# Three of four weight sums on VectorE, and block loads on SyncE's queue, in a Strassen-Winograd feed-forward kernel

## The chip, the cores and the metric

The kernel runs on one NeuronCore of a Trainium2 chip. The metric is device time in microseconds (us) of one execution. Engines: TensorE (PE, with its weight loads as PEld), VectorE (DVE), ScalarE (ACT), GpSimd (POOL) and SyncE (SP, which here only issues DMAs). POOL issues DMAs too, and it alone can issue a DMA that adds to what lies at the destination (an accumulating DMA).

## The reference

An encoder of two layers. Each layer is a feed-forward block, a mixer (gated linear attention beside softmax attention) and a second feed-forward block, on 512 tokens and 16 learned ones (528 columns; 512 in the last block). Everything is float32.

```python
def swiglu(x, w_gate, w_up, w_down):
    return (jax.nn.silu(x @ w_gate) * (x @ w_up)) @ w_down
...
    for l in range(DEPTH):
        h = h + 0.5 * swiglu(rmsnorm(h, norm_gains[l, 0]),
                             ffn_w_gate[l, 0], ffn_w_up[l, 0], ffn_w_down[l, 0])
        h = h + mixer(rmsnorm(h, norm_gains[l, 1]), w_in[l], ...)
        h = h + 0.5 * swiglu(rmsnorm(h, norm_gains[l, 2]),
                             ffn_w_gate[l, 1], ffn_w_up[l, 1], ffn_w_down[l, 1])
    return rmsnorm(h, final_norm)[:, N_META:]
```

D_MODEL is 1024 and D_FF is 2816. The change touches only how the weights of the feed-forward blocks get ready; the mixer's code stays.

## The kernel before

*Layout.* Activations lie transposed, features on the 128 partitions, tokens along the free dimension. A matmul takes a weight tile of 128 x 128 as the stationary operand and half the tokens (264 or 256 columns) as the moving one. To keep float32 accuracy each weight tile and each activation is split in two float32r parts, `hi` (a ScalarE copy, line 259) and `lo` (a VectorE subtraction, line 260), and each product is three matmuls: hi x hi, hi x lo, lo x hi.

*Sets.* A feed-forward block multiplies 2 x 2 blocks by the Strassen-Winograd scheme: seven products, named 1 to 7, where the plain way has eight. The weights of one such scheme are a set `i`: four blocks 11, 12, 21, 22 of 128 x 1024 floats (512 KB) in DRAM (`win`). Products 1, 2 and 4 take the blocks 11, 12 and 22 as they are; the other four take weight sums:

- s3 = B21 - B11, product 7
- s2 = B22 + s3, product 6
- s1 = B21 + B22, product 5
- s4 = s2 - B12, product 3

Of the 15 sets of each of the four feed-forward blocks, 0 to 10 (`NPAIR` = 11) are gate and up ("pairs" of column tiles; line 566 is their matmul), and 11 to 14 are down (line 680). Pairs run in three groups of 4, 4 and 3. After each of the first two groups come two down sets; the third group's down products are done the plain way (line 433).

*How a sum is formed.* `sums` is called when block 11 is fetched (product "1") and when product "2" is made. s3: ScalarE writes -B11 into a "long" buffer (`negative`, line 198), and POOL adds B21 from DRAM by an accumulating DMA (line 203; `s<-win` in the profile). s2: POOL loads B22 into a "short" buffer (line 193, `w<-win`) and adds s3 to it by another accumulating DMA, SBUF to SBUF (`w<-s`). s1: POOL loads B21 into a short buffer and adds B22 from DRAM. s4: in pairs 2 to 10 VectorE subtracts B12 from s2 when product 6 is made (line 228); in the other sets ScalarE negates B12 and POOL adds s2 (`s<-w`). The raw block 12 is kept in its buffer until line 228 has read it.

*Order.* `ffn_steps` writes the products out in order; in the middle of a group it is 1 of the next pair, then 7, then 2 of the next pair, 4, 3, then 6 and 5 of the next pair. `use` makes `hi` and `lo` up to two products ahead and fetches eight ahead. Raw blocks have three buffers and go by SP's queue; long sums have three buffers (`wsa`), short ones two (`wsb`), by POOL's queue. Within these wishes a list scheduler of the compiler sets the order on each engine and queue by its own estimate of times; on the chip each engine and each queue takes its instructions strictly in that order. A line 688 on VectorE adds a finished down product from PSUM to the residual `h` and so frees the bank.

Of the kernel before, what the change touches and what calls it, by code (L numbers as in the profile page):

```python
# [14 lines left out]
ALU = mybir.AluOpType  # L15
# [128 lines left out]
NPAIR = FF // P // 2  # L144
# [21 lines left out]
class Weights:  # L166
# [21 lines left out]
    def block(self, f, i, name, pool=None, tag="raw"):  # L188

        w = (pool or self.raw).tile([P, SLAB], F32, tag=tag, name=f"w{name}_{f[0]}{f[1]}_{i}")  # L190
        first = f + (i, name) == (0, 0, 0, "11")
        for a in np.split(np.arange(SLAB), 2 if first else 1):
            (self.nc.gpsimd if pool else self.nc.sync).dma_start(w[:, a[0] : a[-1] + 1], self.dram(f, i, name)[:, a[0] : a[-1] + 1])  # L193
        return w

    def negative(self, f, i, name, w):
# [8 lines left out]
    def sums(self, f, i, product, w):  # L205


        got = self.summed
        if product == "1":
            s3 = self.negative(f, i, "s3", w)  # L210
            self.add(s3, self.dram(f, i, "21"))
            s2 = self.block(f, i, "22", self.short, "wsb")
            self.add(s2, s3)
            got[f, i, "7"], got[f, i, "6"] = s3, s2
        if product == "12"[(f, i) in OPENING]:
            s1 = self.block(f, i, "21", self.short, "wsb")
            self.add(s1, self.dram(f, i, "22"))
            got[f, i, "5"] = s1
        late = 2 <= i < NPAIR
        if product == "2" and not late:  # L220
            s4 = self.negative(f, i, "s4", w)
            self.add(s4, got[f, i, "6"])
            got[f, i, "3"] = s4
        if product == "2" and late:
            self.kept = w
        if product == "6" and late:
            s4 = self.long.tile([P, SLAB], F32, tag="wsa", name=f"s4_{f[0]}{f[1]}_{i}")
            self.nc.vector.tensor_tensor(s4, w, self.kept, ALU.subtract)
            got[f, i, "3"] = s4
# [15 lines left out]
    def make(self, upto):  # L245
        nc = self.nc
        while self.made < min(upto, len(self.loads)):
            self.fetch(self.made + 1)
            s = self.made
            load = self.loads[s]  # L250
            w = self.raws.pop(s, None)
            if w is None:
                w = self.summed.pop(load)
            hi = self.hi_pool.tile([P, SLAB], F32R, tag="whi", name=f"whi{s}")
            lo = self.lo_pool.tile([P, SLAB], F32R, tag="wlo", name=f"wlo{s}")
            for a in np.split(np.arange(SLAB), 2 if s == 0 else 1):
                cs = slice(a[0], a[-1] + 1)
                with self.tc.issue_after(self.behind) if self.behind else nullcontext():
                    nc.scalar.copy(hi[:, cs], w[:, cs])  # L259
                nc.vector.tensor_tensor(lo[:, cs], w[:, cs], hi[:, cs].bitcast(F32), ALU.subtract)  # L260
            self.got[s] = (hi, lo)
            self.got.pop(s - 12, None)
            self.made += 1
            if not isinstance(load, int) and (load[2] in "26" or load[2] == "1" and load[:2] in OPENING):
                self.sums(*load, w)
# [31 lines left out]
def build(tc, ctx, xt, wts, win, par, w2, const, umask, out):  # L297
    nc = tc.nc
# [16 lines left out]
    def open_pools(side, psum=(), **bufs):  # L315
        made[0] += 1
        out = {}
        for n, b in bufs.items():
            space = dict(space=bass.MemoryType.PSUM) if n in psum else dict(side=side)
            out[n] = tc.alloc_tile_pool(name=f"{n}_{made[0]}", bufs=b, reuse_waits="tile", **space)  # L320
        slots.update(out)
        return out
# [218 lines left out]
    def ffn(l, f, norm, done, following):  # L541

        x, rs, up, n = norm.x, None, None, live[0]
        w = n // 2
        pools = open_pools("left", psum=("s2",), c=4, s2=2)
        made, hid, sums, raw, sets = {}, {}, {}, {}, {}
        risen = iter(range(KC))

# [540 lines left out]
        norm.pools = open_pools("right", **{"x": dict(x=16), "xc": dict(xc=8)}[kind])  # L1089

    def block_pools():
        pools = open_pools("left", wsa=3, wsb=2)
        W.long, W.short = pools["wsa"], pools["wsb"]
        return pools

# [89 lines left out]
    def finish_chunk(c):  # L1185
        fin.square(c)
        gain(c, slice(0, SEQ))

    def ending(sums, operand, rs):

        table("abs_reciprocal_sqrt_and_small")
# [44 lines left out]
    first = Norm(G_NORM)  # L1236
    operand_pools(first, "xc")
    bp = [block_pools()]
    nc.sync.dma_start(h(1), xt[:, 1])
    first.pair(0)  # L1240
# [15 lines left out]
    for l in range(DEPTH):  # L1256
        a, b, c = norms[3 * l : 3 * l + 3]
        ffn(l, 0, a, b.chunk, lambda: operand_pools(b, "x"))
        close_pools(bp.pop())
        mixer(l, b, c.chunk_of_pair, lambda: (operand_pools(c, "xc"), bp.append(block_pools())))  # L1260
        if l < DEPTH - 1:
            d = norms[3 * l + 3]
            ffn(l, 1, c, d.pair_of, lambda: operand_pools(d, "xc"))
        else:
            ffn(l, 1, c, None, lambda: None)
# [72 lines left out]
```

## Time and profile before

| | |
|---|---|
| median of three runs | 2267.75 us (2262.52 to 2270.09) |
| profiled execution | 2280.39 us, span 2278.6 us, mean granted TensorE clock 0.989 |
| PE, PEld busy | 2188.9 us, 2088.3 us |
| DVE, ACT, POOL busy | 1685.8 us, 1262.7 us, 246.1 us |
| w<-win by SP; by POOL | 179 DMAs, median 5.4 us to landing; 180, 6.1 us |
| s<-win, w<-s, s<-w by POOL | 60, 60 and 24 DMAs, median 7.6, 5.2 and 7.7 us to landing |

Busy time is the union of an engine's instructions; what ends an idle time ("<-") is inferred from semaphores. "w" is a loaded block or a short sum, "s" a long sum, "whi" and "wlo" the two parts, "c" and "g" activations of the feed-forward block, "ss" PSUM.

### The profile page before, as it was taken

The numbers are of one execution on the slowest core, as the hardware profiler recorded it, in microseconds if no ns is written. First come the engines' busy times: TensorE is split into PE (matmuls) and PEld (weight loads), VectorE is DVE, ScalarE is ACT, GpSimd is POOL, SyncE is SP. The second block draws the span as 40 slices with busy tenths as digits, with TensorE's granted clock in tenths as the row PEclk, the third lists the DMA queues.
The fourth block names the chain that finished last, engine by engine and source line by source line (L and its number), as shares of the span: only waits on it lengthen the run. The fifth ranks groups of instructions, "written<-read, shape, count | busy, mean of one in ns | idle before, by whom it ended". The sixth has DMA issues, their size and how long they took to land.

```text
span 2278.6 us, 40100 instructions
## 1 busy us (share of the span) xinstructions
PE 2188.9 (96%) x16506; PEld 2088.3 (92%) x16506; DVE 1685.8 (74%) x2607; ACT 1262.7 (55%) x1831; POOL 246.1 (11%) x328
## 2 busy tenths in 40 slices
PE   6989999999999999999999899999999999999998
PEld 6989999989999999998999898998888888999997
DVE  7776867586886678667788768575878767786867
ACT  7545545354785565454575455454547846555553
POOL 1211110000000011111012111100000001121110
PEclk9999999999999999999999999999999999999999
DMA  8877873212113477777668777832121135887871
GB/s 241 217 198 185 203 195 106 77 54 66 47 38 112 129 189 187 204 192 202 175 148 208 201 193 178 201 114 86 56 74 47 47 121 136 216 213 213 204 204 65
DMA packets 94951, 338.68 MB, mean 149 GB/s; under 512 B 10544, under 2 KB 12976, under 8 KB 94768
## 3 DMA queue, kind: packets, MB, share of 16 engines
q0 software_dynamic: 46656, 169.89, 33.9%
q1 hardware_dynamic: 46160, 163.73, 21.2%
q8 instruction: 130, 2.13, 0.4%
q10 hardware_dynamic: 1952, 2.50, 0.3%
q14 instruction: 53, 0.43, 0.1%
HBM read 289.94 MB, written 2.10 MB: 128 GB/s over the span
## 4 chain that ended last, share of the span: by engine, by line
PE 60%; DMA 13%; DVE 12%; issue 8%; ACT 6%; POOL 1%; SPq 0%; DVEq 0%; POOLq 0%; ACTq 0%
PE ss L566 24%; PE mm L433 14%; DMA w<-win 10%; PE ss L433 9%; PE ss L680 4%; DVE wlo L260 3%; PE sm L433 2%; DMA w<-s 2%; ACT whi L259 1%; PE sm L1041 1%; DMA s<-w 1%; PE ss L1016 1%; POOL w L203 1%; ACT s L198 1%; PE sm L1057 1%
## 5 line engine op out<-in xcount | busy, mean ns | idle before, releaser
L566 PE MATMUL ss<-xc,whi 128*128 128x264 f32 (+1 forms) x4928 | 905.6, 285 | 25.6 <-ACT whi L259 13.4
L566 PEld LDWEIGHTS ss<-xc,whi 128*128 128x128 f32 x4928 | 767.1, 189 | 30.8 <-ACT whi L259 14.3
L566 PE MATMUL ss<-xc,wlo 128*128 128x264 f32 (+1 forms) x2464 | 702.1, 285 | 3.7 <-DVE wlo L260 3.7
L260 DVE TENSOR_TENSOR wlo<-w,whi 128x1024 fp32r<-128x1024 f32 (+1 forms) x301 | 365.5, 1217 | 155.6 <-ACT whi L259 155.4
L566 PEld LDWEIGHTS ss<-xc,wlo 128*128 128x128 f32 x2464 | 466.3, 189 | 5.8 <-DVE wlo L260 5.8
L259 ACT CAST whi<-w 128x1024 fp32r<-128x1024 f32 (+1 forms) x301 | 313.0, 1047 | 143.1 <-DMA w<-win 34.0
L433 PE MATMUL mm<-x,whi 128*128 128x264 f32 (+1 forms) x1712 | 385.3, 315 | 0.0
L433 PEld LDWEIGHTS mm<-x,whi 128*128 128x128 f32 x1712 | 279.2, 189 | 16.5 <-issue 1.0
L680 PE MATMUL ss<-g,whi 128*128 128x264 f32 (+1 forms) x1280 | 250.9, 294 | 29.2 <-DVE h L688 17.2
L433 PE MATMUL mm<-x,wlo 128*128 128x264 f32 (+1 forms) x856 | 266.7, 316 | 0.0
L680 PEld LDWEIGHTS ss<-g,whi 128*128 128x128 f32 x1280 | 206.8, 196 | 35.9 <-ACT whi L259 19.5
L259 ACT CAST whi<-raw 128x1024 fp32r<-128x1024 f32 x126 | 132.1, 1049 | 164.4 <-PE mm L433 103.0
L570 ACT COPY c<-ss 128x528 f32<-128x528 f32 (+1 forms) x132 | 78.5, 595 | 224.3 <-PE ss L566 224.1
L260 DVE TENSOR_TENSOR wlo<-raw,whi 128x1024 fp32r<-128x1024 f32 x126 | 153.9, 1222 | 59.3 <-ACT whi L259 58.5
L680 PE MATMUL ss<-g,wlo 128*128 128x264 f32 (+1 forms) x640 | 186.1, 291 | 0.7 <-DVE wlo L260 0.7
L193 POOL DMA_DIRECT2D w<-win x120 | 69.1, 576 | 1079.9 <-DVE x L422 731.2
L260 DVE TENSOR_TENSOR wlo<-s,whi 128x1024 fp32r<-128x1024 f32 x120 | 146.5, 1221 | 43.5 <-ACT whi L259 43.4
L433 PEld LDWEIGHTS mm<-x,wlo 128*128 128x128 f32 x856 | 160.1, 189 | 8.5 <-issue 0.7
L433 PE MATMUL ss<-g,whi 128*128 128x264 f32 (+2 forms) x900 | 166.2, 299 | 0.0
L259 ACT CAST whi<-s 128x1024 fp32r<-128x1024 f32 x120 | 126.1, 1051 | 22.7 <-PE ss L680 15.3
L433 PEld LDWEIGHTS ss<-g,whi 128*128 128x128 f32 x900 | 131.7, 188 | 5.3
L680 PEld LDWEIGHTS ss<-g,wlo 128*128 128x128 f32 x640 | 125.3, 196 | 1.0 <-DVE wlo L260 1.0
(266 smaller groups left out, 3430.8 us busy)
## 6 DMA issues: line engine op xcount, KB each, us to landing
w<-win POOLq DMA_DIRECT2D x180, 512.0 KB, 6.1
w<-win SPq DMA_DIRECT2D x179, 512.0 KB, 5.4
raw<-wts SPq DMA_DIRECT2D x126, 512.0 KB, 3.3
s<-win POOLq DMA_DIRECT2D x60, 512.0 KB, 7.6
w<-s POOLq DMA_DIRECT2D x60, 512.0 KB, 5.2
s<-w POOLq DMA_DIRECT2D x24, 512.0 KB, 7.7
h<-xt SPq DMA_DIRECT2D x3, 528.0 KB, 8.7
out<-h ACTq DMA_DIRECT2D x4, 256.0 KB, 2.3
```

What stands on the lines that cost most here:

```text
L193: (self.nc.gpsimd if pool else self.nc.sync).dma_start(w[:, a[0] : a[-1] + 1], self.dram(f, i, name)[:, a[0] : a[-1] + 1])
L198: self.nc.scalar.activation(t, w, AF.Copy, scale=-1.0)
L203: self.nc.gpsimd.dma_start(t, src, accum_op=ALU.add)
L259: nc.scalar.copy(hi[:, cs], w[:, cs])
L260: nc.vector.tensor_tensor(lo[:, cs], w[:, cs], hi[:, cs].bitcast(F32), ALU.subtract)
L433: TE.matmul(acc.half[i][:width], lhs, rhs[:, acc.spans[i]], start=first, stop=last)
L566: TE.matmul(acc[:, j], a[:, j, k], b[:, at], start=bool(begin and k == 0 and i == 0), stop=k == len(x) - 1 and i == 2, skip_group_check=no ...
L570: W.behind = S.copy(part(st, q), acc).ins
L680: TE.matmul(acc[:, j], a[:, j, k], xs[b][:, k], start=bool(begin and k == 0 and i == 0), stop=k == 3 and i == 2, skip_group_check=not begin)
L1016: TE.matmul(s[:n, i, :HF], lhs, kh[:, hs], start=True, stop=False)
L1041: TE.transpose(tp[:, j * w + u * n : j * w + (u + 1) * n], pr[:n, (2 * c2 + j) * P : (2 * c2 + j + 1) * P], ident[:n, :n])
L1057: TE.matmul(o[:, :w], vw, ph, start=i == 0, stop=False)
```

## The change

Four edits. All block loads go by SP's queue. Short buffers are three instead of two. In gate and up sets 2 to 10 (`plain`), s3's buffer is loaded with B21, and VectorE subtracts B11 from it right after `lo` of product 1; s2's buffer is loaded with B22, and VectorE adds s3 to it when product 2 has been made; with s4, which VectorE formed already, these are three of the four sums, and s1 stays an accumulating DMA. The condition `late` is now `2 <= i` without an upper end, so down sets form s4 on VectorE as well. Pairs 0 and 1 keep the old way for all their sums.

```diff
@@ block
-            (self.nc.gpsimd if pool else self.nc.sync).dma_start(w[:, a[0] : a[-1] + 1], self.dram(f, i, name)[:, a[0] : a[-1] + 1])
+            self.nc.sync.dma_start(w[:, a[0] : a[-1] + 1], self.dram(f, i, name)[:, a[0] : a[-1] + 1])
@@ sums
+        late, plain = 2 <= i, 2 <= i < NPAIR
         if product == "1":
-            s3 = self.negative(f, i, "s3", w)
-            self.add(s3, self.dram(f, i, "21"))
+            if plain:
+                s3 = self.block(f, i, "21", self.long, "wsa")
+            else:
+                s3 = self.negative(f, i, "s3", w)
+                self.add(s3, self.dram(f, i, "21"))
             s2 = self.block(f, i, "22", self.short, "wsb")
-            self.add(s2, s3)
+            if not plain:
+                self.add(s2, s3)
             got[f, i, "7"], got[f, i, "6"] = s3, s2
...
-        late = 2 <= i < NPAIR
...
+        if product == "2" and plain:
+            s3, s2 = got[f, i, "7"], got[f, i, "6"]
+            self.nc.vector.tensor_tensor(s2, s2, s3, ALU.add)
@@ make
             self.got[s] = (hi, lo)
+            if not isinstance(load, int) and load[2] == "1" and 2 <= load[1] < NPAIR:
+                s3 = self.summed[load[:2] + ("7",)]
+                nc.vector.tensor_tensor(s3, s3, w, ALU.subtract)
@@ block_pools
-        pools = open_pools("left", wsa=3, wsb=2)
+        pools = open_pools("left", wsa=3, wsb=3)
```

## The prediction

> **What bounds the kernel now.** I read the page first, then the waits, then the places where TensorE (PE) stood still, in the timeline.
>
> ```profile
> span 2278.6 us, 40100 instructions
> ## 1 busy us (share of the span) xinstructions
> PE 2188.9 (96%) x16506; PEld 2088.3 (92%) x16506; DVE 1685.8 (74%) x2607; ACT 1262.7 (55%) x1831; POOL 246.1 (11%) x328
> ```
>
> TensorE is busy for 96% of the span. A cheaper way to form weight sums therefore gains only where TensorE waits for one, so I looked for these waits (view of all waits: who waited for whom, total us, times, longest):
>
> ```profile
> DVE s L228 <- DMA w<-s: 39.5, 12, 5.9
> ...
> PEld ss L680 <- ACT whi L259: 19.5, 7, 4.5
> PE ss L680 <- DVE h L688: 18.5, 8, 4.3
> ```
>
> VectorE (DVE) stands for 39.5 us in front of L228, the subtraction that makes s4, until the DMA w<-s, which adds s3 to s2, has landed. TensorE waits 19.5 us inside the down products (L680). The timeline of one place joins the two:
>
> ```profile
> 928.30 1.23 DVE L228 TENSOR_TENSOR s<-w,w 128x1024 f32<-128x1024 f32 x1 [4.72 <-DMA w<-s]
> 928.32 1.04 ACT L259 CAST whi<-w 128x1024 fp32r<-128x1024 f32 x1 [0.48 <-DMA w<-s]
> 929.44 0.70 DVE L688 TENSOR_TENSOR h<-h,ss 128x528 f32<-128x528 f32 x1
> 930.06 1.22 DVE L260 TENSOR_TENSOR wlo<-w,whi 128x1024 fp32r<-128x1024 f32 x1
> 930.26 0.30 PEld L680 LDWEIGHTS ss<-g,whi 128*128 128x128 f32 x2 [3.29 <-ACT whi L259]
> 930.29 0.48 PE L680 MATMUL ss<-g,whi 128*128 128x264 f32 x2 [3.10 <-DVE h L688]
> ```
>
> This is the end of the first group's down products. The first gate/up set of the next group (pair 4) has its s2 late; VectorE waits in L228, L688 (which empties the PSUM bank TensorE needs) stands behind it, and TensorE is idle 3.29 us. Why s2 is late, in GpSimd's (POOL) queue:
>
> ```profile
> 912.97 0.86 POOL L203 DMA_DIRECT2D s<-win  x1 [5.44 <-ACT s L198]
> 914.60 0.56 POOL L193 DMA_DIRECT2D w<-win  x1 [0.77 <-DVE h L688]
> 915.86 0.55 POOL L193 DMA_DIRECT2D w<-win  x1 [0.70 <-DVE wlo L260]
> 920.71 0.92 POOL L203 DMA_DIRECT2D w<-s  x1 [4.30 <-DMA w<-win]
> 922.68 0.89 POOL L203 DMA_DIRECT2D w<-win  x1 [1.06 <-DMA w<-win]
> ```
>
> ScalarE's (ACT) negation, the sum from DRAM (912.97), the load of block 22 (914.60, which waited for a short buffer), the sum s2 += s3 (920.71, landed 7.5 us later): one after the other. The same picture stands at five more ends of groups. The idle just ahead of the six is 4.47, 2.39, 3.29, 2.55, 2.44 and 3.13 us, 18.3 together; the 19.5 us row is these and one of 1.20. What follows each idle, beside one undisturbed set (columns: stretch, length, busy us and count per engine, granted clock, DMA share, GB/s):
>
> ```profile
> 838.60:859.10 20.50, 20.50 (x170) 20.50 (x169) 14.14 (x18) 9.94 (x13) 2.88 (x4) 1.00 0.89 224
> 158.79:165.79 7.00, 7.00 (x39) 7.00 (x40) 3.44 (x4) 0.00 (x0) 0.56 (x1) 0.65 0.91 253
> 292.31:299.31 7.00, 7.00 (x45) 7.00 (x46) 3.44 (x4) 0.00 (x0) 0.56 (x1) 0.76 1.00 266
> 930.29:937.29 7.00, 7.00 (x45) 7.00 (x46) 3.44 (x4) 0.00 (x0) 0.56 (x1) 0.76 0.92 233
> 1064.42:1071.42 7.00, 7.00 (x45) 7.00 (x46) 3.44 (x4) 0.00 (x0) 0.56 (x1) 0.76 0.92 262
> 1299.78:1306.78 7.00, 7.00 (x45) 7.00 (x46) 3.44 (x4) 0.00 (x0) 0.56 (x1) 0.76 0.92 255
> 1437.16:1444.16 7.00, 7.00 (x46) 7.00 (x47) 3.45 (x4) 0.00 (x0) 0.57 (x1) 0.77 1.03 275
> 52.40:59.40 7.00, 7.00 (x37) 7.00 (x38) 5.58 (x8) 3.83 (x5) 1.11 (x2) 0.61 1.03 218
> ```
>
> The undisturbed set does 170 matmuls in 20.50 us, 0.1206 us each, at clock 1.00 with no idle: the sums cost TensorE nothing there. After each of the six the clock is 0.65 to 0.77, and 265 matmuls are done in the six stretches where 348 would fit: 83 x 0.1206 = 10.0 us more. So a stall here costs about one and a half times its length. The last row is the start of the kernel: 21 matmuls missing, 2.5 us, behind this idle of 4.5 us:
>
> ```profile
> 51.04 0.49 PEld L566 LDWEIGHTS ss<-xc,whi 128*128 128x128 f32 x2 [3.73 <-ACT whi L259]
> 52.30 0.29 PEld L566 LDWEIGHTS ss<-xc,wlo 128*128 128x128 f32 x1 [0.77 <-DVE wlo L260]
> ```
>
> **The change part by part.**
>
> ```profile
> L198 ACT ACTIVATE s<-w 128x1024 f32<-128x1024 f32 x84 | 88.6, 1057 | 66.9 <-DMA w<-win 55.1 <-DVE wlo L260 11.5
> ...
> L228 DVE TENSOR_TENSOR s<-w,w 128x1024 f32<-128x1024 f32 x36 | 43.9, 1221 | 39.5 <-DMA w<-s 39.5
> ```
>
> Counts. Sets 2 to 10 of four feed-forward blocks are 36 plain sets. In each, ScalarE's negation and two accumulating DMAs (s3 from DRAM, s2 += s3) go; a plain load and two VectorE operations come. The new test for "late" has lost its upper bound, so the 16 down sets also make s4 on VectorE, without negation and DMA. ScalarE loses 36 + 16 = 52 operations of 1.057 us (55 us), POOL 88 accumulations of its 204, VectorE gains 72 + 16 = 88 of 1.221 us (107 us).
>
> *The six stalls.* The chain for pair 4 becomes two loads and two VectorE operations. With three short buffers block 22 need not wait for one of two, so it may be asked for before 914.60; even issued there it was there by 920.71 (the next step of the queue began then), and the 7.5 us of the DMA sum become 1.2. By these s2 is ready before 926 (estimated: 920.71, two operations, and some queueing), L228 finds it, and L688 is not held. Gain 18.3 + 10.0 = 28.3 us. Ends: all of it, or half, if something next in line (s1, which stays an accumulation, issued at 922.68) is late. I take all, since s2 has more than 2 us to spare at 928.
>
> *The start.* Pairs 0 and 1 keep their accumulations, but the third buffer lets pair 1's block 22 come earlier, and two loads of pair 0 move behind the first activations in SP's queue. Ends: 4.5 + 2.5 = 7.0 gained; 6.1 lost (a load in line, 914.60 to 920.71). I take 4 gained, since the wait at 51.04 ended with a sum that a buffer delayed.
>
> *VectorE's 72 in the plain sets.* Of the 20.50 us of a set it is busy 14.14; two more make 16.6 and leave 3.9. The idle places in that set:
>
> ```profile
> 853.37 1.23 DVE L260 TENSOR_TENSOR wlo<-s,whi 128x1024 fp32r<-128x1024 f32 x1 [1.33 <-ACT whi L259]
> 854.51 1.22 DVE L260 TENSOR_TENSOR wlo<-w,whi 128x1024 fp32r<-128x1024 f32 x1
> 859.20 1.23 DVE L260 TENSOR_TENSOR wlo<-w,whi 128x1024 fp32r<-128x1024 f32 x1 [3.47 <-ACT whi L259]
> ```
>
> s2 += s3 stands behind the wlo of 854.51, in the 3.47 us; s3 -= w some us earlier, ahead of the 1.33. Both are covered. Ends: nothing, or 72 x 1.22 = 88 us with the cover gone; I take 3, for the eight first sets of a group, where an L688 may wait behind one (8 x 1.14, a third of it).
>
> *VectorE's 16 in the down sets.* These land where it is dense and TensorE waits for it:
>
> ```profile
> 897.66 1.31 DVE L688 TENSOR_TENSOR h<-h,ss 128x528 f32<-128x528 f32 x2
> 898.94 1.26 DVE L642 TENSOR_TENSOR c<-g,c 128x1056 fp32r<-128x1056 f32 x1
> 900.12 1.22 DVE L260 TENSOR_TENSOR wlo<-w,whi 128x1024 fp32r<-128x1024 f32 x1
> ```
>
> There is no idle between these rows, so a subtraction ahead of them shifts L642 by its 1.2 us. Ends: 0 and 16 x 1.22 = 19.5. I take 6, about a third: half of them stand at the second half of a down stage, where weights are made ahead.
>
> *ScalarE's 52 and POOL's 88.* Neither bounds; gain 0, at most the 1.20 us left in the 19.5 row.
>
> *The queue.* SP issues 156 loads more: 120 from POOL, 36 new. One issue:
>
> ```profile
> 906.30 0.33 SPq L193 DMA_DIRECT2D w<-win  x1
> ```
>
> 156 x 0.33 = 51 us over the whole span on an engine that computes nothing: 0. What waits behind a load that has no buffer yet is the slower rival.
>
> Sum: -18.3 - 10.0 - 4 + 3 + 6 = -23.3 us. The profiled run took 2280.39 us (its span and 1.8 around it), 0.56% over the median of 2267.75; scaled, 2267.75 x (2280.39 - 23.3) / 2280.39 = 2244.6, so 2245.
>
> The 10.0 us come from the clock column. The Trainium skill, page "TensorE: Matmul & The Clock Gate", section "HAM oscillation — how this bites in real kernels", gives the rule as no idle of TensorE longer than about 3.4 us. By it only the first of the six, 4.47 us, would be followed by a slow clock. The trace differs: idle of 2.39 us was, too.
>
> **The rivals.**
>
> *Next in line.* Half of the 28.3 us stays, because s1 or a down-stage operand is late at the same place. For: s1's sum was issued last, at 922.68. Against: TensorE needs it two products later. -23.3 + 14.2 = -9.1: 2259.
>
> *The slow clock stays.* The stretch after a group's end is slow even without the idle; only the idle goes. Against: all six slow stretches follow an idle and the undisturbed set has clock 1.00. -13.3: 2254. The rule of that page of the Trainium skill would take 7.7 of the 10.0 us from the sum, which gives about the same time.
>
> *It does not do what it says.* Fewer accumulations, the same waits elsewhere: 2268.
>
> *Slower: SP's queue holds up the blocks.* Place: the eight starts of a group.
>
> ```profile
> SPq L193 <- DVE wlo L260: 808.2, 116, 18.4
> ```
>
> SP already stands 7.0 us a time for a buffer (808.2 / 116); now loads for two more pools stand in the same line, and a down set's block 12 keeps its raw buffer until s4 is formed. In the trace that buffer came free with a negation, and the load of 906.30 took it. If the first blocks of a group come 7.0 us late and TensorE waits for them, 8 x 7.0 = 56 us: -23.3 + 56 = +33, 2300. It decides from 23.3 / 8 = 2.9 us each. Against: none of the waits of TensorE in the rows above is for such a block. The Trainium skill, page "DMA: Bandwidth & Descriptors", section "Queues, rings and completion order", says that an engine takes a ring's descriptors in order and alternates between rows; no run here shows whether the urgent block loses by leaving POOL's row unused.
>
> *Slower: VectorE stalls.* s3 -= w reaches the front before block 21 has landed, in all 36 sets. From 23.3 / 36 = 0.65 us of it on TensorE each it decides; with 1.2 each, +20: 2288. Against: block 21 is issued right behind 11, far ahead.
>
> **How the numbers follow.** Chances: my forecast, 2230 to 2256, 0.42; next in line 0.16; slow clock 0.10; no change 0.07; SP's queue 0.16; VectorE's stall 0.09. Within 0.3% (7 us) is what these runs can't tell from no change. Faster 0.68, same 0.07, slower 0.25. The range reaches down to 2226, where the start gives its 7.0 and the down sets cost nothing with a few us to spare, and up to 2290, into the slower cases; about 2 in 10 is left out. The forecast's own range is 2230 to 2256.
>
> **What would show it.** Right: no L680 idle over 1.5 us behind L228 at the ends of groups, clock 1.00 after them, the wait "DVE s L228 <- DMA w<-s" gone from plain sets, undisturbed sets still 20.5 us with VectorE near 16.6. Wrong: TensorE waiting for whi at the first products of a group while SP waits for buffers; VectorE waiting for w<-win ahead of the new line; waits for L642 grown by well over 6 us; an undisturbed set longer than 20.5 us.

## The result, and the profile after

The changed kernel takes 2245.19 us (median of four runs, 2243.20 to 2249.32); the kernel before, run on the same chip, takes 2267.18 us (2262.52 to 2270.09). The ratio is 0.9907, with a 95% interval of 0.9885 to 0.9930: faster, by 22 us. The forecast was 2245, so the total is right. Most of its terms are not, as the accounting below shows.

The page of the changed kernel, in the same order as the prediction read the one of before:

```profile
span 2247.4 us, 40053 instructions
## 1 busy us (share of the span) xinstructions
PE 2178.9 (97%) x16506; PEld 2081.2 (93%) x16506; DVE 1781.4 (79%) x2695; ACT 1210.3 (54%) x1779; POOL 101.7 (5%) x120
```

The instruction counts are those of the prediction: VectorE has 88 more, ScalarE 52 fewer, and POOL has lost its 120 loads and 88 accumulating DMAs. Next, the view of all waits (who waited for whom, total us, times, longest), with the lines of VectorE and TensorE that answer to those of before:

```profile
DVE w L271 <- DMA w<-win: 54.0, 18, 6.0
...
ACT whi L266 <- DMA w<-win: 3.3, 5, 1.4
```

The wait "DVE s L228 <- DMA w<-s" (39.5 us) is gone. VectorE now waits in L271, the new s3 -= w, for the load of block 21: 54.0 us in 18 of the 36 sets. In the other direction, ScalarE's waits in the line that makes `hi` (259 before, 266 after) for a DMA into a block or short sum fell to 3.3 us; before they were 34.0:

```profile
ACT whi L259 <- DMA w<-win: 34.0, 20, 5.8
```

At the six group ends, the stretches that begin with the same weight load as in the prediction's table (columns as there; VectorE is the third pair):

```profile
154.77:161.77 7.00, 7.00 (x60) 7.00 (x59) 6.31 (x7) 1.87 (x3) 0.00 (x0) 1.00 0.58 208
283.20:290.20 7.00, 7.00 (x60) 7.00 (x59) 6.32 (x7) 1.89 (x3) 0.00 (x0) 1.00 0.59 204
913.98:920.98 7.00, 7.00 (x60) 7.00 (x59) 6.33 (x7) 1.84 (x3) 0.00 (x0) 1.00 0.60 216
...
1394.12:1401.12 7.00, 7.00 (x60) 7.00 (x59) 6.31 (x7) 1.86 (x3) 0.00 (x0) 1.00 0.57 189
```

Each now holds 60 records where before it held 39 to 46, at clock 1.00, with no idle ahead. That part went as forecast.

**Where the time went.** TensorE runs the same 16506 matmuls in both kernels, and in the same order but for seven places of at most 66 weight loads within which some change places. So the start of the k-th weight load can be compared directly. The difference to before, in us, summed over four kinds of stretch (start: up to 71.6 us of before; group ends: 60 weight loads on either side of each of the six; last block: from 1946 us of before; between: all the rest). The rows below the first are the experiments told further on; each is the profiled execution against that of before:

```
                 start  group ends  between  last block   total
prediction        -4.0    -28.3       +9.0       0        -23.3
changed kernel    +2.5    -28.2      -19.5     +13.9      -31.4
queue_buffer      -7.6    -28.2      -13.3      +9.7      -39.4
queue_only        -8.2    -10.2       -3.6      +3.9      -18.0
buffer_only       -2.4    -28.3      -10.6      +5.0      -36.3
sums_alone        +3.4    -28.2      +22.1     +20.5      +17.9
two_short         -2.0    -28.2       +8.3     +21.6       -0.5
qb_late           -6.8    -23.5      -12.8     +14.5      -28.5
late_bound        +0.3    -28.2      -12.8      +7.5      -33.2
down_too          -2.0    -28.2       +3.9      +4.1      -22.2
qb_make           -7.0    -26.2      -15.6      -4.5      -53.3
after_make        -1.8    -28.2      -17.6      -5.8      -53.4
```

These are differences of single executions. The profiled execution of before (2280.39 us) lies 13 us over its median and that of the changed kernel (2249.32) 4 over its own, so the total of the changed kernel's row is about 9 us larger than the medians' difference (and queue_only's execution, 2262.47, lies 10 over its median). Where those 9 us sit was not found; a term of a few us in the table is therefore only an indication, and the verdicts go by the timed rounds.

The new loss, in the last feed-forward block, in the timeline of the changed kernel:

```profile
1946.03 0.88 POOL L203 DMA_DIRECT2D w<-s  x1 [5.61 <-DMA w<-win]
1946.66 1.14 POOL L203 DMA_DIRECT2D w<-win  x1
...
1948.56 2.33 SPq L193 DMA_DIRECT2D w<-win  x2
...
1955.84 1.06 ACT L198 ACTIVATE s<-w 128x1024 f32<-128x1024 f32 x1 [6.15 <-DMA w<-win]
1956.80 0.81 ACT L651 CAST c<-g 128x768 fp32r<-128x768 f32 x1
1957.30 0.86 POOL L203 DMA_DIRECT2D s<-win  x1 [9.50 <-ACT s L198]
1957.52 0.58 ACT L580 COPY c<-ss 128x512 f32<-128x512 f32 x1
...
1958.15 0.30 PEld L576 LDWEIGHTS ss<-xc,whi 128*128 128x128 f32 x2 [4.87 <-ACT c L580]
```

ScalarE stands 6.15 us in L198, the negation of a down set's block 11, because that block, issued at 1948.56, came 7 us later. Behind it in ScalarE's order stands L580, a snapshot of PSUM that frees the bank for TensorE; so TensorE stands still for about 5 us at 1958.15, and again at 2090.66 for the second pair of down sets (5.40 us of idle, negation at 2088.34 with 6.68 of waiting). Before, the order on ScalarE was the same, but the block came in 4 us:

```profile
1993.88 2.33 SPq L193 DMA_DIRECT2D w<-win  x2
1993.90 0.90 POOL L203 DMA_DIRECT2D w<-s  x1 [6.27 <-DMA w<-win]
1994.86 0.89 POOL L203 DMA_DIRECT2D w<-win  x1
...
1997.85 1.06 ACT L198 ACTIVATE s<-w 128x1024 f32<-128x1024 f32 x1 [2.85 <-DMA w<-win]
```

In the changed kernel two accumulating DMAs (1946.03, 1946.66) were issued ahead of that load; before, the same two were issued just after it (1993.90, 1994.86). The other runs whose negation stands at this place agree. In the eleven traces with it there are 22 such loads, two in each. At five of them (both of before, both of sums_alone, the second of queue_only) the first accumulating DMA was issued at most 0.22 us ahead and the second behind, and the load landed after 3.6 to 4.3 us; at the other 17 the first was issued 0.7 to 2.5 us ahead, and it took 5.6 to 8.0. No run changes this order alone, so it is a strong correlation and not a proof.

### The profile page after: what moved, and what is told of

It reads as the page before. It is cut to its first block, busy times and chain, and to the rows that moved or that the text cites. A ratio compares the mean times of both kernels' runs of the same rounds, so it can differ in the third digit from the quotient of the medians.

```text
span 2247.4 us, 40053 instructions
## 1 busy us (share of the span) xinstructions
PE 2178.9 (97%) x16506; PEld 2081.2 (93%) x16506; DVE 1781.4 (79%) x2695; ACT 1210.3 (54%) x1779; POOL 101.7 (5%) x120
## 5 line engine op out<-in xcount | busy, mean ns | idle before, releaser
L267 DVE TENSOR_TENSOR wlo<-w,whi 128x1024 fp32r<-128x1024 f32 (+1 forms) x337 | 407.3, 1217 | 81.0 <-ACT whi L266 80.9
L266 ACT CAST whi<-w 128x1024 fp32r<-128x1024 f32 (+1 forms) x337 | 348.2, 1048 | 167.9 <-PE ss L690 73.3
L690 PE MATMUL ss<-g,whi 128*128 128x264 f32 (+1 forms) x1280 | 239.7, 286 | 4.6 <-DVE h L698 3.1
L690 PEld LDWEIGHTS ss<-g,whi 128*128 128x128 f32 x1280 | 198.6, 188 | 9.2 <-ACT whi L266 3.5
L580 ACT COPY c<-ss 128x528 f32<-128x528 f32 (+1 forms) x132 | 78.4, 594 | 227.5 <-PE ss L576 227.4
L690 PE MATMUL ss<-g,wlo 128*128 128x264 f32 (+1 forms) x640 | 181.1, 283 | 0.0
L443 PEld LDWEIGHTS ss<-g,whi 128*128 128x128 f32 x900 | 131.7, 188 | 5.3
L203 POOL DMA_DIRECT2D w<-win x60 | 54.6, 910 | 1586.4 <-DVE wlo L267 754.4
L690 PEld LDWEIGHTS ss<-g,wlo 128*128 128x128 f32 x640 | 120.5, 188 | 0.0
L422 ACT ACTIVATE c<-c 128x528 f32<-128x528 f32 (+1 forms) x88 | 56.5, 642 | 114.5 <-DVE c L620 114.4
L690 PE MATMUL ss<-c,whi 128*128 128x264 f32 (+1 forms) x512 | 102.8, 295 | 9.9 <-DVE c L652 9.4
```

The lines of the kernel that those rows point to most:

```text
L203: self.nc.gpsimd.dma_start(t, src, accum_op=ALU.add)
L422: prev_act[0] = S.activation(*args, **kw).ins
L443: TE.matmul(acc.half[i][:width], lhs, rhs[:, acc.spans[i]], start=first, stop=last)
L580: W.behind = S.copy(part(st, q), acc).ins
L690: TE.matmul(acc[:, j], a[:, j, k], xs[b][:, k], start=bool(begin and k == 0 and i == 0), stop=k == 3 and i == 2, skip_group_check=not begin)
```

## The experiments

Each was timed in three rounds beside the kernel before. The first three ask which of the four edits did it.

**queue_buffer.** The kernel before with SP's queue and the third short buffer, and no new VectorE operation.

```diff
-            (self.nc.gpsimd if pool else self.nc.sync).dma_start(w[:, a[0] : a[-1] + 1], ...)
+            self.nc.sync.dma_start(w[:, a[0] : a[-1] + 1], ...)
...
-        pools = open_pools("left", wsa=3, wsb=2)
+        pools = open_pools("left", wsa=3, wsb=3)
```

> The kernel before with SyncE's queue and the third short buffer alone; all sums as before. Theory A (the six stalls are the late s2 at the start of a group, a chain of buffer, load and two accumulating DMAs): the buffer goes, but s2 += s3 still waits for s3's sum and takes 7.5 us itself, so s2 comes some 2 us earlier and about half of the 28 us is gained: near 2253 us, the six stalls shorter but there. Rival B (the buffer and the queue are the whole of it): 2240 to 2247. Rival C (only fewer accumulations count): 2267 within 4.

Measured: 2239.64 us, ratio 0.9876 (0.9848 to 0.9903). All six stalls are gone, without any of the 72 operations that were to shorten the chain. The changed kernel's 2245.19 is, if anything, slower.

**sums_alone.** The changed kernel's VectorE sums, with POOL's queue and two short buffers as before (both lines above undone).

> VectorE's sums with POOL's queue for the loads and two short buffers. Theory A: block 22 of a group's first pair is loaded from 914.6 to 920 as before, two VectorE operations of 1.2 us follow, s2 is ready before 928: the six stalls are gone, near 2245 us. Rival B (buffer and queue): stalls stay, 2260 or more. A third way: a load waiting for one of two short buffers now stops VectorE in its order; then new VectorE waits ahead of the two new lines and 2250 to 2265.

Measured: 2296.21 us, ratio 1.0120 (1.0101 to 1.0139): slower than before. The six stalls go here as well, so the shorter chain is real. But new waits come in their place:

```profile
DVE w L271 <- DMA w<-win: 63.4, 12, 7.4
DVE w L232 <- DMA w<-win: 60.8, 23, 5.0
PEld ss L576 <- DVE wlo L267: 36.3, 36, 4.2
PEld ss L576 <- ACT whi L266: 21.6, 15, 9.2
```

VectorE waits in both new operations for a load, the wlo of another product stands behind it, and TensorE waits for that.

**late_bound.** The changed kernel with down sets' s4 made as before.

```diff
-        late, plain = 2 <= i, 2 <= i < NPAIR
+        late = plain = 2 <= i < NPAIR
```

> The changed kernel, but down sets form s4 by negation and accumulating DMA again (16 VectorE operations fewer, 16 negations and 16 accumulations more). The prediction's term says 6 us faster: 2239. By the trace after, the waits for line 652 did not grow, so theory A now says within 4 us of 2245. Rival (keeping block 12's raw buffer until s4 is formed is what makes block 11 late in the last feed-forward block): 8 to 14 us faster, 2231 to 2237, all of it in the last block.

Measured: 2248.84 us, ratio 0.9913 (0.9891 to 0.9935). Undoing that part gains nothing; the 6 us that the prediction charged for it are not there. In the last block TensorE still stands still twice (5.62 and 3.82 us), so the rival, the longer hold of block 12's buffer, is not what makes block 11 late there. This kernel is also queue_buffer with the 72 new VectorE operations and nothing else, and it is 9 us slower than that run (the two intervals just overlap).

**neg_behind.** The changed kernel with the negation to be issued behind the snapshot, by the compiler's ordering hint.

```diff
+        with self.tc.issue_after(self.behind) if self.behind else nullcontext():
             self.nc.scalar.activation(t, w, AF.Copy, scale=-1.0)
```

> The changed kernel, with each negation on ScalarE placed behind the newest snapshot (the same rule as the whi copies have). Theory A for the 14 us lost in the last feed-forward block: a negation waits 6 us for block 11 and holds the snapshot behind it; then that block loses its two long stalls of 5 to 5.6 us and the slow clock behind them: 2231 to 2235. Rival (block 11 is late because SP's queue holds it up, and what needs it would wait anyway): within 4 us of 2245.

Measured: 2251.79 us, ratio 0.9924 (0.9906 to 0.9943), with idle of 5.23 and 5.71 us still in the last block. The hint named a snapshot that was already past, so the order on ScalarE stayed. The run tells nothing of the cause.

**queue_only** and **buffer_only.** The two lines of queue_buffer, one at a time.

> The kernel before with the block loads on SyncE's queue, two short buffers. Together with the third buffer this gave 2239.6. Theory D (the buffer is what counts: block 22 of a group's first pair no longer waits for the two sums ahead of it to be used): little here, 2262 to 2270, the six stalls still there; a load that waits for a buffer can now also hold up raw blocks, then slower than 2270. Rival E (the queue counts: on POOL's queue a load stands in line behind accumulating DMAs and their waits): 2245 or less, the six stalls gone.

> The kernel before with three short buffers, loads still on POOL's queue. Theory D: the six stalls are gone, 2240 to 2248. Rival E: 2260 or more, the loads still wait in POOL's line; both in part: between.

Measured: queue_only 2252.03 us, ratio 0.9919 (0.9891 to 0.9947); buffer_only 2247.71, ratio 0.9896 (0.9865 to 0.9927). With the queue alone the picture at the group ends is still that of before, shorter:

```profile
146.53 1.23 DVE L228 TENSOR_TENSOR s<-w,w 128x1024 f32<-128x1024 f32 x1 [3.67 <-DMA w<-s]
...
147.67 0.70 DVE L688 TENSOR_TENSOR h<-h,ss 128x528 f32<-128x528 f32 x1
...
148.48 0.30 PEld L680 LDWEIGHTS ss<-g,whi 128*128 128x128 f32 x2 [2.25 <-ACT whi L259]
```

With the buffer alone all six are gone (28.3 us in the table). So the third short buffer is what releases the stalls; the queue adds the start, where queue_only and queue_buffer gain 8 us and buffer_only 2.

**two_short.** The changed kernel with two short buffers.

```diff
-        pools = open_pools("left", wsa=3, wsb=3)
+        pools = open_pools("left", wsa=3, wsb=2)
```

> The changed kernel with two short buffers. Queue alone left the six stalls, buffer alone removed them, sums alone on POOL's queue removed them too but cost elsewhere. Theory G (either the buffer or the short chain does it): no L690 idle over 2.4 us at the ends of groups, but VectorE waits longer for block 22, 2250 to 2265. Rival (only the buffer does it): the six stalls back, 2265 or more. If VectorE's waits were the queue's doing alone: 2245.

Measured: 2277.92 us, ratio 1.0034 (1.0016 to 1.0052), slower than before and further from the changed kernel than expected. The group ends are clean, as in sums_alone, but the plain sets are not:

```profile
L576 PEld LDWEIGHTS ss<-xc,wlo 128*128 128x128 f32 x2464 | 469.5, 191 | 35.3 <-DVE wlo L267 35.1
...
L271 DVE TENSOR_TENSOR w<-w,w 128x1024 f32<-128x1024 f32 x36 | 44.0, 1222 | 85.1 <-DMA w<-win 85.1
L232 DVE TENSOR_TENSOR w<-w,w 128x1024 f32<-128x1024 f32 x36 | 44.0, 1222 | 28.9 <-DMA w<-win 28.7
```

L271 waits 85.1 us and L232 28.7. In the changed kernel these are 54.0 and 0.6:

```profile
L271 DVE TENSOR_TENSOR w<-w,w 128x1024 f32<-128x1024 f32 x36 | 44.0, 1222 | 54.0 <-DMA w<-win 54.0
L232 DVE TENSOR_TENSOR w<-w,w 128x1024 f32<-128x1024 f32 x36 | 44.0, 1222 | 0.6
```

The third buffer thus matters more with the sums on VectorE (33 us between this median and the changed kernel's) than without (12 us between queue_only and queue_buffer, 23 between buffer_only and before).

**qb_late.** queue_buffer with s4 of the down sets on VectorE (`late = 2 <= i`).

> Queue and third buffer alone, and down sets form s4 on VectorE (the changed kernel's third part by itself). The prediction's term of 6 us lost says 2246. The run without this part of the changed kernel was 3.6 us slower than with it, so theory now: 2235 to 2240. Rival: the longer hold of block 12's raw buffer makes the last block worse, 2243 or more.

Measured: 2249.80 us, ratio 0.9899 (0.9867 to 0.9932): 10 us slower than queue_buffer, where I had expected it to gain or hold. VectorE waits there for the accumulating DMA that makes s2, once at each of the eight ends of down products (first at 151.53, last at 2144.85, 5.7 to 7.5 us each); the changed kernel has the same DMA in the down sets and no such wait:

```profile
DVE s L228 <- DMA w<-s: 50.2, 8, 7.5
```

Two of the eight are in the last block. The negations there wait no longer than in queue_buffer (6.62 and 6.78 us against 6.57 and 6.90), so the time fits the rival (2243 or more), but its mechanism does not show. So this edit costs some 10 us beside the old sums and nothing beside the new ones. Why the DMA is in time in the latter is open.

**down_too.** The changed kernel with s3 and s2 of the down sets on VectorE as well.

```diff
-        late, plain = 2 <= i, 2 <= i < NPAIR
+        late = plain = 2 <= i
...
-            if not isinstance(load, int) and load[2] == "1" and 2 <= load[1] < NPAIR:
+            if not isinstance(load, int) and load[2] == "1" and 2 <= load[1]:
```

> The changed kernel with s3 and s2 of the down sets on VectorE as well: no negation is left but those of pairs 0 and 1, so none can hold a snapshot in the last block. Theory A: that block's 13 us return, 2232; but the subtraction now stands on VectorE in front of dense work at the ends of groups and waits there for block 21, as at the start: 0 to 25 us lost. So 2232 to 2257, above 2245 if VectorE's order is the dearer one. Rival (VectorE has room for it): 2232 or less.

Measured: 2258.43 us, ratio 0.9953 (0.9934 to 0.9972), 13 us slower than the changed kernel. The long stalls of the last block are gone, since no negation is left there, but in its place each of the six earlier down stages has an idle of 1.8 us and the two in the last block one of 2.6. The first of them, and the 7 us behind it:

```profile
125.11 1.04 ACT L266 CAST whi<-s 128x1024 fp32r<-128x1024 f32 x1
125.20 1.31 DVE L698 TENSOR_TENSOR h<-h,ss 128x528 f32<-128x528 f32 x2
126.01 0.50 PEld L690 LDWEIGHTS ss<-g,whi 128*128 128x128 f32 x2 [1.79 <-ACT g L651]
```

```profile
125.80:132.80 7.00, 6.41 (x26) 5.89 (x27) 7.00 (x8) 2.41 (x3) 0.00 (x0) 0.51 0.02 2
```

VectorE is busy for the whole 7.00 us of that stretch, in the dense place that the prediction charged 6 us for. But none of the sums (L232, L235, L271) stands among VectorE's rows from 119 to 132 us, and the compiler also ordered TensorE's products of the down stages otherwise than in the changed kernel (966 weight loads stand elsewhere than before, 198 there). Whether the three sums per down set or this order makes the idle was not separated.

**qb_make** and **after_make.** These test the reading of the last block. In its down sets, `sums` is called when product 1 is made, by which time block 11 has been loaded, and no longer when it is fetched; ScalarE then does not stand in front of a load. The edit is the same in queue_buffer (qb_make) and in the changed kernel (after_make).

```diff
+    def at_make(self, load):
+        return load[:2] in OPENING or load[0] == (1, 1) and load[1] >= NPAIR
...
-                if load[2] == "1" and load[:2] not in OPENING:
+                if load[2] == "1" and not self.at_make(load):
...
-            if not isinstance(load, int) and (load[2] in "26" or load[2] == "1" and load[:2] in OPENING):
+            if not isinstance(load, int) and (load[2] in "26" or load[2] == "1" and self.at_make(load)):
```

> Queue and third buffer alone (2239.6), and in the down sets of the last feed-forward block alone the negation of block 11 is asked for when that block is made, not when it is fetched. Theory A (there the negation waits for block 11 on ScalarE with a snapshot behind it): the two stalls of 5.5 and 5.8 us and the slow clock behind them go, 10 to 13 us: 2227 to 2230. Rival (block 11 is late for its first use anyway): within 4 us of 2239.6. If s3 is now late for product 7, slower.

> The changed kernel, and in the down sets of the last feed-forward block the negation of block 11 is asked for when that block is made (the edit that gave 13.5 us on queue and buffer alone). Theory A: the same two stalls of 5 to 5.6 us and their slow clock go here too: 2245 - 13 = 2232, within 4. Rival (in the changed kernel it is the longer hold of block 12's raw buffer): 2241 or more.

Measured: qb_make 2226.10 us, ratio 0.9798 (0.9770 to 0.9825), 13.5 us better than queue_buffer; after_make 2229.42, ratio 0.9820 (0.9781 to 0.9859), 16 better than the changed kernel. In qb_make the same place reads so:

```profile
1945.59 1.05 ACT L262 CAST whi<-w 128x1024 fp32r<-128x1024 f32 x1
1947.94 0.59 ACT L573 COPY c<-ss 128x512 f32<-128x512 f32 x1 [1.30 <-PE ss L569]
...
1951.06 1.06 ACT L198 ACTIVATE s<-w 128x1024 f32<-128x1024 f32 x1 [0.64 <-DVE wlo L263]
```

The snapshot (here L573) waits for nothing but TensorE's own product, and the negation follows it. The cause of the last block's loss is shown, then: the place of the negation in ScalarE's order, ahead of a snapshot, with a load that comes late. The edit also moves the set's other loads and accumulating DMAs, which are asked for with the negation, so the order on ScalarE and the traffic changed together; why the load comes late stays open. qb_make and after_make are the fastest versions of this study, 2% under the kernel before, and their intervals overlap.

**after_start.** The changed kernel with pairs 2 and 3 of the first block formed the old way, since the two waits of L271 at the start (4.02 us at 51.32, 6.04 us at 67.52) belong to them.

```diff
+    def plain(self, f, i):
+        return (4 if f == (0, 0) else 2) <= i < NPAIR
...
-        late, plain = 2 <= i, 2 <= i < NPAIR
+        late, plain = 2 <= i, self.plain(f, i)
```

> The changed kernel with pairs 2 and 3 of the first feed-forward block formed the old way (negation and accumulating DMAs), the other 34 plain sets on VectorE. Theory F: at the start VectorE waits 4.0 and 6.0 us in the subtraction for block 21, and TensorE loses 10 us against queue and buffer alone there: 2235 to 2238. Rival (the start is slow from the traffic of the loads, whoever sums): within 4 us of 2245.

Measured: 2242.80 us, ratio 0.9874 (0.9842 to 0.9907). In the trace the start gains: at 71.6 us the difference to before is -5.4 us, where the changed kernel has +2.5. The median moves by 2.4 us only, within what the runs can tell from nothing; so the trace shows the mechanism, and the time does not confirm its 8 us.

## Why the prediction was right, and where it was not

*The six stalls: right in place and size.* Predicted 28.3 us, 28.2 in the trace. The prediction also counted a slow clock behind each stall (10.0 of the 28.3) against the rule of the Trainium skill, page "TensorE: Matmul & The Clock Gate", section "HAM oscillation — how this bites in real kernels", by which only idle above about 3.4 us would count. The idle that went was 18.3 us and the gain is 28.2, so the trace's reading held. The rival "the slow clock stays" falls with it, and "next in line" too: s1 was not late.

*But it credited the wrong part.* The step on the six stalls said that the chain becomes two loads and two VectorE operations, with the buffer as a help. Either remedy is enough for these six places (buffer_only and sums_alone both have 28), but only the buffer comes without new waits. Beside the queue and the buffer, the sums on VectorE add nothing: 2245.19 with them, 2239.64 without, and 2248.84 with the 72 of the plain sets alone. Had the change been the sums alone, the same working would have forecast a gain, and the kernel is 26 us slower.

*The start: wrong sign, 6.5 us.* Predicted -4, measured +2.5. The early idle went (-6.6 us at 56 us of before), but pairs 2 and 3 have L271, and their block 21 came late while the kernel's first loads were in flight. This is the rival "VectorE stalls", here in two sets where it had been priced for 36. The reason given against it, that block 21 is issued far ahead, does not hold: in 18 of the 36 sets VectorE waited for it, which was one of the signs named for being wrong. Only one wait outside the start is followed by an idle of TensorE over 1 us (4.42 us at 196.69, idle of 1.35 at 200.36). The two at the start:

```profile
51.32 1.23 DVE L271 TENSOR_TENSOR w<-w,w 128x1024 f32<-128x1024 f32 x1 [4.02 <-DMA w<-win]
...
54.35 0.29 PEld L576 LDWEIGHTS ss<-xc,wlo 128*128 128x128 f32 x1 [3.94 <-DVE wlo L267]
```

*VectorE's operations, +3 and +6: too dear, and the other way about.* The undisturbed plain set shows the cover that was named:

```profile
827.10:847.60 20.50, 20.50 (x171) 20.50 (x170) 16.76 (x21) 9.84 (x13) 0.88 (x1) 1.00 0.52 154
```

20.50 us, VectorE 16.76 where 16.6 was worked out, no idle on TensorE. Between the group ends the kernel did not lose 9 us; it gained 19.5. The prediction had put ScalarE's and POOL's part at 0, at most 1.20 us. At three down stages alone, from the weight loads at 1023.39, 1258.90 and 1390.37 of before on, the difference grows by 3.0, 4.0 and 4.6 us. Two waits of ScalarE stand behind these. First, before, ScalarE stood 34.0 us in front of L259 for a DMA "w<-win". By the DMA that ended each wait, 31.6 of these were waits for s1, the sum that stays an accumulating DMA: its DMA was the last of its set in POOL's queue. TensorE paid for some of it, for instance here:

```profile
1256.20 1.05 ACT L259 CAST whi<-w 128x1024 fp32r<-128x1024 f32 x1 [5.81 <-DMA w<-win]
1257.28 1.23 DVE L260 TENSOR_TENSOR wlo<-w,whi 128x1024 fp32r<-128x1024 f32 x1 [6.24 <-ACT whi L259]
...
1258.90 0.30 PEld L680 LDWEIGHTS ss<-c,whi 128*128 128x128 f32 x2 [2.21 <-DVE g L620]
```

The DMA that ended the 5.81 us was issued by POOL at 1246.16 and landed at 1256.12. VectorE, held by the late wlo, is late with what TensorE waits for at 1258.90. I had looked at the waits for s2 and s4 only, and had even asked whether s1 would be late at the six places, not whether it was late elsewhere. Second, the place at 1390.37, whose 1.20 us the prediction did name, is the last block's mechanism: a down set's negation waits for its block, and the copy to `hi` that TensorE needs stands behind it.

```profile
1388.33 1.06 ACT L198 ACTIVATE s<-w 128x1024 f32<-128x1024 f32 x1 [6.11 <-DMA w<-win]
...
1390.37 0.30 PEld L680 LDWEIGHTS ss<-g,whi 128*128 128x128 f32 x2 [1.20 <-ACT whi L259]
```

With 0.96 us more of idle at 1391.63 and a clock of 0.76 over the 7 us from 1390.37, that is the step of 4.6 us. In the changed kernel the same negation waits less, and no idle of TensorE over 1 us follows:

```profile
1350.82 1.06 ACT L198 ACTIVATE s<-w 128x1024 f32<-128x1024 f32 x1 [2.11 <-DMA w<-win]
```

queue_buffer has most of the gain between the group ends too (13.3), so it is not the VectorE sums that brought it. The three steps are 11.6 of the 19.5 us; the rest was not traced. Nor does the length of the waits give the gain: queue_only cut those for s1 to 9.5 us and has 3.6 in this column.

*The last block, +13.9: not in any term.* ScalarE's and POOL's changes were costed at nothing because neither bounds. But the seed was in the trace of before, the 2.85 us of L198 at 1997.85, ahead of a snapshot. It was the rival "SP's queue holds up the blocks" in another shape: not the eight group starts, and not a load issued later (it was issued 1.1 us ahead of the place where ScalarE began to wait, before as after), but one load that takes 7 us instead of 4 in front of an in-order ScalarE.

The errors, +6.5, -28.5 and +13.9 with the right term kept, sum to -8.1, which is the difference between the profiled -31.4 and the forecast's -23.3; in the medians (-22.0) it does not show. The total came out right because the three errors partly cancelled and the two profiles lie differently to their medians. That is luck; what the prediction had right is the six stalls and their clock.

## What to carry to other kernels

Where a stall has two remedies, more room for what is late or less work to make it, price them apart: here either one released all six stalls, but the moved sums added waits of their own, and beside the buffer they gained nothing. On an engine that works strictly in order, an instruction that waits for a load delays all that stands behind it, however idle the engine is on average, so look at what follows each such wait, and put the instruction where its data have already come. Count every row in which an engine waits for a load, not only those named after the operation that is changed.

## What the runs showed of the hardware

Short idle of TensorE can be followed by a slow clock: 2.39 us at one group end was (granted clock 0.76 over the next 7 us), and in down_too idle of 1.79 us on the weight loads was (0.51). Not each idle near 2 us is: at 1027.58 of before 1.93 us was followed by none (1.00), so no threshold can be given from these runs. In qb_make, which has no slow stretch but the one at its very end, the mean granted clock is 0.998, against 0.989 before.

The same 512 KB load took 4 us from issue to the end of the wait in one kernel (1993.88 to 1997.85) and 7.3 in another (1948.56 to 1955.84). At this place of eleven traces it took 3.6 to 4.3 us when the two accumulating DMAs were issued with it or behind it, and 5.6 to 8.0 when at least one was issued 0.7 us or more ahead. Whether these DMAs are the cause was not isolated.
